# A hybrid decoder layer on one core: the delta rule's products and output turn in another order, w_out's gate on another engine, and a PSUM pool of its own for the last norm

## The chip, the core and the metric

The kernel runs on one core of a Trainium2 chip. The core has five engines, each with an instruction queue of its own that it works through in order: TensorE (PE in the profile; PEld is its weight load), VectorE (DVE), ScalarE (ACT), GpSimd (POOL) and SyncE (SP), which here issues most of the transfers (DMA). [...] The metric is device time in microseconds of one execution, as a median of runs.

## The reference, cut to what matters

One layer over 2048 tokens of width 1024: a combined projection, two mixers (a short convolution and a gated delta rule with 4 heads of 128), an output product with w_out, a layer norm, 32 experts of which each token takes two, and a last layer norm. All in float32.

```python
h = x * (1 + scale1) + shift1
proj = h @ w_in                       # 1024 x 3592
y_conv = short_conv_mixer(...)        # 512 columns
y_dn = gated_deltanet(...)            # 512 columns: the delta rule below, then RMS norm, times silu(z)
x = layer_norm(ALPHA * x + gate1 * (concat(y_conv, y_dn) @ w_out), ln1_g, ln1_b)
x = layer_norm(ALPHA * x + gate2 * hierarchical_moe(x * (1 + scale2) + shift2), ln2_g, ln2_b)

def step(S, xs):                      # one chunk of the delta rule, for each head
    delta = u_c - w_c @ S
    o = qd_c @ S + qk_c @ delta
    S = S * dec_c + ke_c^T @ delta
    return S, o
```

## The kernel before, in words

The mixer works in two halves of 1024 tokens. In each half the projections run column tile by column tile (`qkv_tile`, `z_tile`, `conv_group`); each product is split in three fp32r matmuls (line 283). The delta rule's 16 chunks of 128 tokens go by generators that `drive` steps beside the projections: each `yield` of the main line lets a side generator make a fixed share of a step (0.6 in the first half, 1.0 in the second). `gdn` runs `gdn_a` for the half's 8 chunks, then an inversion (`gdn_inv`, `gdn_merge`), then `gdn_b` chunk by chunk, which carries the state S. The second half's chunks run on beside `mix_tile`, which makes the w_out product and the first norm for 128 tokens at a time; `main` makes it wait until `gdn_done` has passed its chunk.

Outside the blocks marked `manual_schedule`, the order in which the code is written gives each instruction a rank, and a planner, which knows costs and due times of its own, puts the instructions of each engine in their final order before anything runs. So two generators' instructions are mixed on each queue, and an instruction can be planned well ahead of its place. Buffers are given out by the planner too: the tiles of `t2` share 11 buffers (m2), the PSUM tiles of `gps` share 4 banks.

In `gdn_b` a chunk loads six tiles (kTb, qTb, Tm, qkb, keb, veb) and later szb. For each head, PE makes pr = k S (line 719), and DVE forms r in veb from it (line 720). PE multiplies T by r into pdl (line 723), ACT scales that to e in Tm (line 726), PE makes ke e into pS (line 730) and DVE the new state from it (line 732). The output o in qTb is q S (line 739, ACT line 741) plus qk e (line 745, DVE line 748). Then follow a sum of squares on ACT (line 754), a chain of small DVE instructions for the root (lines 755 to 759), a scaling of qTb (line 761), four transposes on PE into oT (line 768), a product with szb on DVE (line 769) and a store (line 770). Lines 719 and 720 alternate by head within one PSUM bank, and so do lines 730 and 732.

`load_wout` loads w_out in eight pieces, multiplies each by the gate on POOL (line 827) and splits it on ACT and DVE (lines 828 and 829). This runs beside the last `conv_group` of the second half and the first tiles of the mix.

`moe` runs the experts under an order written by hand for all engines. Its PSUM tiles come from the pools ph (1 bank) and pk (7 banks), which stay open to the end. `tail` is the last norm over 16 tiles of 128 tokens, in six groups (`TAIL`); only SP's order is by hand there. For each tile, ACT normalises the columns from TS on (line 1649), POOL multiplies and adds the norm's rows there (line 1657), and DVE does all of the first TS columns in two instructions (line 1656), with the rows g and b taken from PSUM (the banks of pT, 512 columns each, filled at line 1585). TS is 512.

Of the kernel before, what the change touches and what calls it, by code (L numbers as in the profile page):

```python
# [10 lines left out]
F32 = mybir.dt.float32  # L11
# [5 lines left out]
OP = mybir.AluOpType  # L17
# [3 lines left out]
P = 128  # L21
D = 1024
# [5 lines left out]
H = 4  # L28
# [7 lines left out]
NG = 4  # L36
NONE = 1 << 20
ADA = 0.4
TS, TAIL = 512, ((1, 1), (2, 1), (3, 1), (4, 1), (3, 1), (3, 1))
HS = 608  # L40

RA, RB, MH2, MH3, WO = 0.6, 1.0, 0.25, 0.5, 0.5
# [7 lines left out]
def dram(ap, offset, dims):  # L50
    return bass.AP(tensor=ap.tensor, offset=ap.offset + offset, ap=[list(d) for d in dims])


class Layer:
# [647 lines left out]
    def gdn_b(self, ci):  # L702
# [13 lines left out]
        if ci:  # L716
            pr = self.gps("pr")
            for h in range(H):
                nc.tensor.matmul(pr[:, h * P:(h + 1) * P], kT[:, h], S[:, h], start=True, stop=True)
                nc.vector.scalar_tensor_tensor(r[:, h], pr[:, h * P:(h + 1) * P], self.neg_eg[:, ci, h:h + 1], r[:, h], op0=OP.mult, op1=OP.add)  # L720
            yield
        for h in range(H):
            nc.tensor.matmul(pd[:, h * P:(h + 1) * P], T[:, h], r[:, h], start=True, stop=True)
        e = T
# [3 lines left out]
        pS = self.gps("pS")  # L728
        for h in range(H):
            nc.tensor.matmul(pS[:, h * P:(h + 1) * P], ke[:, h], e[:, h], start=True, stop=True)  # L730
            if ci:
                nc.vector.scalar_tensor_tensor(Sn[:, h], S[:, h], self.dec[:, ci, h:h + 1], pS[:, h * P:(h + 1) * P], op0=OP.mult, op1=OP.add)
            else:
                nc.vector.tensor_copy(Sn[:, h], pS[:, h * P:(h + 1) * P])
# [27 lines left out]
        sz = self.t2((P, H, P), name="szb")  # L762
        q, off = divmod(ci, 4)
        nc.sync.dma_start(sz, dram(self.szT[q], off * P, [[QW, P], [P * QW, H], [1, P]]))
        yield
        pT = self.gps("oT")
        for h in range(H):
            nc.tensor.transpose(pT[:, h * P:(h + 1) * P], o[:, h], self.ident)
        nc.vector.scalar_tensor_tensor(fl(sz), pT, self.dnw, fl(sz), op0=OP.mult, op1=OP.mult)
        nc.sync.dma_start(dram(self.yT[q], 4 * P * QW + off * P, [[QW, P], [P * QW, H], [1, P]]), sz)  # L770
        yield

    def scratch(self):
# [40 lines left out]
    def load_wout(self):  # L814

        nc, I = self.nc, self.I
        g1 = self.xp.tile([P, D], F32, tag="x", name="gate1")
        self.row(g1, self.d_mod, 0)
        self.wo = []
        for n in range(2):  # L820
            c = slice(n * 512, n * 512 + 512)
            lo = self.t16([P, KD, 512], F32R, name="wo_lo")
            hi = self.t16([P, KD, 512], F32R, name="wo_hi")
            for k in range(0, KD, 2):
                r = self.raw4((P, 2, 512), name="wo_raw")
                nc.sync.dma_start(r, dram(I["w_out"], k * P * D + n * 512, [[D, P], [P * D, 2], [1, 512]]))
                nc.gpsimd.tensor_tensor(r, r, g1[:, None, c].to_broadcast([P, 2, 512]), op=OP.mult)
                nc.scalar.activation(hi[:, k:k + 2], r, AF.Copy)
                nc.vector.tensor_tensor(lo[:, k:k + 2], r, hi[:, k:k + 2].bitcast(F32), op=OP.subtract)
                yield  # L830
            self.wo.append((hi, lo))
            while not self.second:
                yield
# [327 lines left out]
    def moe_pools(self, st):  # L1161
        p = lambda **k: self.pool(st, **k)
        self.raws.append(p(name="raw8b", bufs=3))
        self.yp = p(name="yp", bufs=3)
        self.xtp = p(name="xtp", bufs=2)
        self.hp = p(name="hp", bufs=3)
        self.hrp = p(name="hrp", bufs=2)
        self.mc = p(name="mc", bufs=1)
        self.small = p(name="small2", bufs=2)
        self.ph = p(name="ph", bufs=1, space=PSUM)  # L1170
        self.pk = p(name="pk", bufs=1, space=PSUM)

    def load_up(self, e):

# [400 lines left out]
    def tail(self):  # L1575
# [4 lines left out]
        junk, stats = (self.hrp.tile([P, D], F32, tag="hr", name=n) for n in ("junk", "stats"))  # L1580
        xs, groups = [], []

        rows = [t.rearrange("p a b -> p (a b)") for t in self.pTs]
        for t, r in zip(rows, (g, b)):
            act.activation(t, r[:, 0:TS], AF.Copy)
        for i in range(NT // 4):
# [3 lines left out]
                nc.sync.dma_start(x[:, j], self.d_xa[t * P:(t + 1) * P])  # L1590
                xs.append(x[:, j])

        t, cols = 0, self.pgs[0]
        for n, nv in TAIL:
            f = stats[:, 64 * len(groups):64 * len(groups) + 64]
            c = cols[:, 16 * len(groups):16 * len(groups) + 16]
# [145 lines left out]
    def gdn(self, half):  # L1742
        c0 = 8 * half
        for c in range(8):
            yield from self.gdn_a(c0 + c)
        yield from self.gdn_inv(half)
        yield from self.gdn_merge(c0)
        for c in range(c0, c0 + 8):
            yield from self.gdn_b(c)
            self.gdn_done = c + 1  # L1750
            if c % 2 == 0 and c < c0 + 6:
                yield from self.gdn_merge(c + 2)

    def step(self, x):
        try:
# [2 lines left out]
            self.sides.remove(x)  # L1758

    def drive(self):  # L1760
        self.sides, self.later, self.gdn_done = [], [], 0
        for _ in self.main():
            for x in list(self.sides):
                x.append(x.pop() if len(x) > 2 else 0.0)
# [7 lines left out]
    def run(self):  # L1772
# [16 lines left out]
        with self.late as st:  # L1789
            self.moe_pools(st)  # L1790
            E = mybir.EngineType
            with self.tc.manual_schedule(engines={E.PE, E.Activation, E.DVE, E.Pool, E.SP}):
                self.moe()
            with self.tc.manual_schedule(engines={mybir.EngineType.SP}):
                self.tail()


# [17 lines left out]
```

## Time and profile before

| what | value |
|---|---|
| median of 3 runs | 1762.85 us (1756.54, 1763.17, 1762.85) |
| profiled execution | 1759.53 us |
| its span, first to last instruction | 1757.8 us |
| mean granted clock of TensorE | 0.954 |
| busy: PE, DVE, ACT, POOL | 88%, 72%, 44%, 31% |
| mixer, to the last mix tile | 0 to about 1163 us |
| experts | about 1193 to 1674 us |
| last norm | about 1674 to 1757.8 us |

Busy time is an average over these stages. A wait is the idle time of an engine ahead of an instruction, with the instruction that ended it. [...]

### The profile page before, as it was taken

What the parts mean: (1) busy time and instruction counts of PE and PEld (TensorE: products, weight loads), DVE (VectorE), ACT (ScalarE), POOL (GpSimd) and SP (SyncE); (2) the same over time, 40 slices, a digit from 0 to 9 for tenths busy, and PEclk for the clock granted to TensorE, in tenths of its full rate; (3) what the DMA queues carried; (4) which work ended last, traced back from release to release, by engine and by line L of the source; (5) the groups of instructions that cost most, each with busy time, mean ns of one, the idle gap of its engine ahead of it and who ended that gap; (6) DMA issues with size and microseconds to landing.
All of it is one profiled execution on the core that took longest, in us unless ns stands there. A gap on an engine that the chain in (4) does not pass through costs nothing. (4 is left out here: it accounts for less than half of the span.)

```text
span 1757.8 us, 25239 instructions
## 1 busy us (share of the span) xinstructions
PE 1555.2 (88%) x7786; PEld 1265.9 (72%) x7786; DVE 1259.4 (72%) x3042; ACT 774.6 (44%) x1604; POOL 537.5 (31%) x442
## 2 busy tenths in 40 slices
PE   5899999998999999999789999958999989999800
PEld 4678877877777778888668888846777778778600
DVE  6777667766877987684678878786666786776554
ACT  4433445445233336444443332235545565554452
POOL 3200111021110002122321121225656675765427
PEclk9999999999999999999899999978999999999955
DMA  9553586456765758544477764449989998998464
GB/s 282 168 184 102 165 248 198 128 138 164 211 202 149 216 162 249 147 98 121 134 231 222 238 204 145 139 150 269 291 256 289 289 327 253 299 300 243 107 221 179
DMA packets 348006, 356.79 MB, mean 203 GB/s; under 512 B 49745, under 2 KB 283842, under 8 KB 347858
## 3 DMA queue, kind: packets, MB, share of 16 engines
q1 hardware_dynamic: 330610, 316.63, 57.4%
q0 software_dynamic: 17248, 38.37, 9.1%
q8 instruction: 70, 1.15, 0.3%
q14 instruction: 78, 0.64, 0.1%
HBM read 268.84 MB, written 101.79 MB: 211 GB/s over the span
## 5 line engine op out<-in xcount | busy, mean ns | idle before, releaser
L283 PE MATMUL acc<-hhi,w_hi 128*128 128x512 f32 x896 | 363.2, 406 | 7.8 <-ACT st L447 3.4
L283 PE MATMUL acc<-hlo,w_hi 128*128 128x512 f32 x896 | 358.2, 400 | 2.3 <-DVE hlo L340 1.3
L283 PE MATMUL acc<-hhi,w_lo 128*128 128x512 f32 x896 | 359.1, 401 | 0.0
L283 PEld LDWEIGHTS acc<-hhi,w_hi 128*128 128x128 f32 x896 | 172.1, 192 | 45.4 <-ACT st L447 4.4
L283 PEld LDWEIGHTS acc<-hlo,w_hi 128*128 128x128 f32 x896 | 171.7, 192 | 38.1 <-DVE hlo L340 2.7
L283 PEld LDWEIGHTS acc<-hhi,w_lo 128*128 128x128 f32 x896 | 172.0, 192 | 35.9 <-issue 1.7
L1223 POOL TENSOR_TENSOR dn<-dn_raw,dn 128x1024 fp32r<-128x1024 f32 x64 | 168.3, 2659 | 59.3 <-ACT dn L1222 57.0
L1214 DVE TENSOR_TENSOR gu_lo<-gu_raw,gu_hi 128x1024 fp32r<-128x1024 f32 (+1 forms) x128 | 172.8, 1393 | 15.4 <-ACT gu_hi L1213 8.5
L1256 PE MATMUL pg<-gu_hi,xT_hi 128*128 128x512 f32 x376 | 150.0, 399 | 0.7 <-ACT xT_hi L1246 0.5
L1256 PE MATMUL pg<-gu_hi,xT_lo 128*128 128x512 f32 x376 | 147.5, 392 | 0.1
L1256 PE MATMUL pg<-gu_lo,xT_hi 128*128 128x512 f32 x376 | 147.2, 392 | 0.0
L1289 PE MATMUL pd<-dn,hT_hi 128*128 128x512 f32 x376 | 120.7, 402 | 6.3 <-PEq L1332 3.2
L1213 ACT ACTIVATE gu_hi<-gu_raw 128x1024 fp32r<-128x1024 f32 (+1 forms) x128 | 125.1, 1035 | 1.9
L456 DVE SCALAR_TENSOR_TENSOR cv<-st,cw,cv 128x512 f32<-128x512 f32 x144 | 108.6, 754 | 2.0
L1303 POOL DMA_INDIRECT d_xa<-y,idx x47 | 77.0, 1638 | 103.8 <-DVEq L1332 44.2
L917 PE MATMUL mix<-wo_hi,y_hi 128*128 128x512 f32 x256 | 104.1, 407 | 1.3 <-ACT y_hi L876 1.3
L917 PE MATMUL mix<-wo_hi,y_lo 128*128 128x512 f32 x256 | 103.2, 403 | 1.3 <-DVE y_lo L878 1.3
L917 PE MATMUL mix<-wo_lo,y_hi 128*128 128x512 f32 x256 | 102.0, 398 | 0.0
L350 ACT ACTIVATE w_hi<-raw 128x1024 fp32r<-128x1024 f32 x56 | 59.6, 1065 | 89.2 <-PE acc L283 70.4
L1247 DVE TENSOR_TENSOR xT_lo<-pT,xT_hi 128x512 fp32r<-128x512 f32 x94 | 60.6, 686 | 40.0 <-ACT xT_hi L1246 34.5
L578 POOL TENSOR_SCALAR_AFFINE_SELECT gam<-gam 128x512 f32<-128x512 f32 x16 | 10.8, 675 | 250.0 <-ACT gam L577 202.7
L1289 PEld LDWEIGHTS pd<-dn,hT_hi 128*128 128x128 f32 x376 | 67.1, 188 | 27.4 <-issue 7.0
(364 smaller groups left out, 3276.8 us busy)
## 6 DMA issues: line engine op xcount, KB each, us to landing
dn_raw<-in_w_down_dram SPq DMA_DIRECT2D x32, 1024.0 KB
gu_raw<-in_w_gate_dram SPq DMA_DIRECT2D x60, 512.0 KB
gu_raw<-in_w_up_dram SPq DMA_DIRECT2D x60, 512.0 KB
raw<-in_w_in_dram SPq DMA_DIRECT2D x56, 512.0 KB
ada_w<-in_w_ada_dram SPq DMA_DIRECT2D x96, 256.0 KB
qkvT<-cv SPq DMA_DIRECT2D x48, 256.0 KB
x_t<-in_x_dram SPq DMA_DIRECT2D x16, 512.0 KB
y_raw<-yT SPq DMA_DIRECT2D x16, 512.0 KB
```

The source lines that it names most:

```text
L283: self.nc.tensor.matmul(ps, a[:, k, :], b[q][:, k, :], start=k + n == 0, stop=k == KD - 1 and n == 2)
L350: nc.scalar.activation(hi, raw, AF.Copy)
L456: nc.vector.scalar_tensor_tensor(y, st[:, t:t + 512], self.cw4[:, j, t:t + 1], y, op0=OP.mult, op1=OP.add)
L578: nc.gpsimd.affine_select(gam, gam, pattern=[[0, H], [1, P]], compare_op=OP.is_ge, fill=0.0, base=0, channel_multiplier=-1)
L917: self.nc.tensor.matmul(ps, a[:, k, :], self.wo[n][b][:, k, :], start=k + i == 0, stop=k == KD - 1 and i == 2)
L1213: nc.scalar.activation(hi[:, c], r, AF.Copy)
L1214: i = nc.vector.tensor_tensor(lo[:, c], r, hi[:, c].bitcast(F32), op=OP.subtract)
L1223: nc.gpsimd.tensor_tensor(dn[:, 1, k], r[:, k], dn[:, 0, k].bitcast(F32), op=OP.subtract)
L1247: nc.vector.tensor_tensor(lo[:, c], pT[n], hi[:, c].bitcast(F32), op=OP.subtract)
L1256: self.nc.tensor.matmul(ps, a[:, k], b[:, k], start=n == 0, stop=n == 3 * KD - 1)
L1289: self.nc.tensor.matmul(ps[n], hT[a][:, k], dn[:, b, k, c], start=i == 0, stop=i == 5)
L1303: i = self.nc.gpsimd.indirect_dma_start(out=self.d_xa, out_offset=bass.IndirectOffsetOnAxis(ap=idx[:, 0:1], axis=0), in_=y, in_offset=None ...
```

## The change

It has five parts. In `gdn_b` the four heads' products of lines 719 and 730 are written together, ahead of the four DVE instructions that read them. The output turn (transposes, product, store) becomes a function that is put on a list; the next chunk calls it after its own pr and ahead of pdl, and the half's last one is called at the end of `gdn`; the mark `gdn_done` is set inside it. `gdn` makes 4 (first half) or 2 (second half) empty steps ahead of its first `gdn_b`. `load_wout` multiplies by the gate on DVE instead of POOL. And the pools ph and pk are closed after `moe`; the last norm takes its rows (two banks each) and its small columns (one bank) from a PSUM pool of its own, with TS 704 instead of 512.

```diff
-TS, TAIL = 512, ((1, 1), (2, 1), (3, 1), (4, 1), (3, 1), (3, 1))
+TS, TAIL = 704, ((1, 1), (2, 1), (3, 1), (4, 1), (3, 1), (3, 1))
...
             for h in range(H):
                 nc.tensor.matmul(pr[:, h * P:(h + 1) * P], kT[:, h], S[:, h], start=True, stop=True)
+            for h in range(H):
                 nc.vector.scalar_tensor_tensor(r[:, h], pr[:, h * P:(h + 1) * P], self.neg_eg[:, ci, h:h + 1], r[:, h], op0=OP.mult, op1=OP.add)
             yield
+        while self.gdn_out:
+            self.gdn_out.pop()()
         for h in range(H):
             nc.tensor.matmul(pd[:, h * P:(h + 1) * P], T[:, h], r[:, h], start=True, stop=True)
...
         for h in range(H):
             nc.tensor.matmul(pS[:, h * P:(h + 1) * P], ke[:, h], e[:, h], start=True, stop=True)
+        for h in range(H):
             if ci:
                 nc.vector.scalar_tensor_tensor(Sn[:, h], S[:, h], self.dec[:, ci, h:h + 1], pS[:, h * P:(h + 1) * P], op0=OP.mult, op1=OP.add)
...
-        yield
-        pT = self.gps("oT")
-        for h in range(H):
-            nc.tensor.transpose(pT[:, h * P:(h + 1) * P], o[:, h], self.ident)
-        nc.vector.scalar_tensor_tensor(fl(sz), pT, self.dnw, fl(sz), op0=OP.mult, op1=OP.mult)
-        nc.sync.dma_start(dram(self.yT[q], 4 * P * QW + off * P, [[QW, P], [P * QW, H], [1, P]]), sz)
+
+        def out():
+            pT = self.gps("oT")
+            for h in range(H):
+                nc.tensor.transpose(pT[:, h * P:(h + 1) * P], o[:, h], self.ident)
+            nc.vector.scalar_tensor_tensor(fl(sz), pT, self.dnw, fl(sz), op0=OP.mult, op1=OP.mult)
+            nc.sync.dma_start(dram(self.yT[q], 4 * P * QW + off * P, [[QW, P], [P * QW, H], [1, P]]), sz)
+            self.gdn_done = ci + 1
+        self.gdn_out.append(out)
         yield
...
-                nc.gpsimd.tensor_tensor(r, r, g1[:, None, c].to_broadcast([P, 2, 512]), op=OP.mult)
+                nc.vector.tensor_tensor(r, r, g1[:, None, c].to_broadcast([P, 2, 512]), op=OP.mult)
...
-        rows = [t.rearrange("p a b -> p (a b)") for t in self.pTs]
+        rows = [self.pk.tile([P, D], F32, name=f"row{i}")[:, 0:TS] for i in range(2)]
...
-        t, cols = 0, self.pgs[0]
+        t, cols = 0, self.pk.tile([P, 512], F32, name="cols")
...
         yield from self.gdn_merge(c0)
+
+        for _ in range(4 if half == 0 else 2):
+            yield
         for c in range(c0, c0 + 8):
             yield from self.gdn_b(c)
-            self.gdn_done = c + 1
             if c % 2 == 0 and c < c0 + 6:
                 yield from self.gdn_merge(c + 2)
+        while self.gdn_out:
+            self.gdn_out.pop()()
...
-            with self.tc.manual_schedule(engines={E.PE, E.Activation, E.DVE, E.Pool, E.SP}):
-                self.moe()
-            with self.tc.manual_schedule(engines={mybir.EngineType.SP}):
+            with ExitStack() as banks:
+                self.ph = self.pool(banks, name="ph", bufs=1, space=PSUM)
+                self.pk = self.pool(banks, name="pk", bufs=1, space=PSUM)
+                with self.tc.manual_schedule(engines={E.PE, E.Activation, E.DVE, E.Pool, E.SP}):
+                    self.moe()
+            self.pk = self.pool(st, name="pt", bufs=1, space=PSUM)
+            with self.tc.manual_schedule(engines={E.SP}):
                 self.tail()
```

## Rows read from the trace of the kernel before

**Rows 1.** The page, part 1: busy us, share of span, instructions.

```profile
PE 1555.2 (88%) x7786; PEld 1265.9 (72%) x7786; DVE 1259.4 (72%) x3042; ACT 774.6 (44%) x1604; POOL 537.5 (31%) x442
```

**Rows 2.** Stretches: length; busy PE, PEld, DVE, ACT, POOL; PE clock, DMA share, GB/s.

```profile
420.00:660.00 240.00, 225.57 (x1173) 179.16 (x1173) 196.99 (x528) 86.31 (x242) 20.75 (x29) 0.98 0.65 189
...
830.00:905.00 75.00, 60.35 (x281) 48.89 (x281) 50.17 (x96) 32.01 (x61) 26.01 (x18) 0.86 0.54 160
...
1200.00:1674.00 474.00, 447.28 (x2141) 359.38 (x2139) 324.98 (x401) 254.53 (x369) 290.71 (x152) 1.00 0.86 267
...
1702.00:1757.80 55.80, 0.00 (x0) 0.00 (x0) 30.93 (x112) 24.27 (x38) 39.59 (x32) 0.50 0.43 173
```

**Rows 3.** PE's waits, whole span: us in total, times, longest.

```profile
PE oT L768 <- DVE qTb L761: 11.6, 8, 4.2
...
PE pS L730 <- DVE S L732: 4.6, 3, 3.3
...
PE pr L719 <- DVE veb L720: 2.9, 3, 1.9
PE pdl L723 <- DMA veb<-d_ve: 2.3, 1, 2.3
```

**Rows 4.** The same view, 420 to 660 us only.

```profile
PE oT L768 <- DVE qTb L761: 6.1, 6, 2.5
```

**Rows 5.** Timeline of PE, 830 to 870: start, length, instructions, [idle before, its end].

```profile
838.44 0.49 PE L719 MATMUL pr<-S,kTb 128*128 128x128 f32 x2 [1.89 <-DVE veb L720]
...
850.51 0.79 PE L730 MATMUL pS<-Tm,keb 128*128 128x128 f32 x2 [3.28 <-DVE S L732]
...
863.66 0.37 PE L768 MATMUL oT<-ident,qTb 128*128 128x128 f32 x1 [4.18 <-DVE qTb L761]
```

**Rows 6.** Timelines of POOL and of DVE in the same stretch.

```profile
833.18 2.41 POOL L827 TENSOR_TENSOR wo_raw<-wo_raw,gate 128x1024 f32<-128x1024 f32 x1 [0.84 <-DMA wo_raw<-in_w_out_dram]
...
844.46 4.66 POOL L827 TENSOR_TENSOR wo_raw<-wo_raw,gate 128x1024 f32<-128x1024 f32 x2 [2.99 <-DMA wo_raw<-in_w_out_dram]
858.77 4.75 POOL L827 TENSOR_TENSOR wo_raw<-wo_raw,gate 128x1024 f32<-128x1024 f32 x2 [9.65 <-DVE rst L124]
...
833.47 3.21 DVE L829 TENSOR_TENSOR wo_lo<-wo_raw,wo_hi 128x1024 fp32r<-128x1024 f32 x1 [3.39 <-ACT wo_hi L828]
...
846.76 2.65 DVE L490 TENSOR_SCALAR cy<-st,cw 128x512 f32<-128x512 f32 x1
...
858.92 2.24 DVE L759 TENSOR_TENSOR om<-ors,aq 128x4 f32<-128x4 f32 x1
...
882.76 0.48 DVE L490 TENSOR_SCALAR cy<-st,cw 128x512 f32<-128x512 f32 x1
```

**Rows 7.** Groups by line: busy us, mean ns, idle before with releasers.

```profile
L352 DVE TENSOR_TENSOR w_lo<-raw,w_hi 128x1024 fp32r<-128x1024 f32 x52 | 63.5, 1222 | 18.4 <-ACT w_hi L350 17.3 <-PE xT L327 1.0
```

**Rows 8.** Lines L768 and L917: shortest, median, longest ns; first and last start.

```profile
L768 PE MATMUL oT<-ident,qTb x64: 270/327/477, 438.8 to 1045.0; 128*128 128x128 f32 x64
...
L917 PE MATMUL mix<-wo_hi,y_lo x256: 387/389/628, 893.3 to 1163.2; 128*128 128x512 f32 x128
```

**Rows 9.** Timelines of POOL and DVE in the last norm.

```profile
1719.15 32.42 POOL L1657 TENSOR_TENSOR tail_x<-tail_x,ln 128x512 f32<-128x512 f32 x26 [3.36 <-ACT tail_x L1649]
...
1733.14 0.15 DVE L1644 TENSOR_TENSOR stats<-pg,stats 128x3 f32<-128x3 f32 x1
```

**Rows 10.** Groups by line, as in rows 7.

```profile
L809 POOL TENSOR_TENSOR rows<-rows,rowt 128x1024 f32<-128x1024 f32 x1 | 2.4, 2399 | 9.9 <-DVE rowt L807 9.9
...
L1657 POOL TENSOR_TENSOR tail_x<-tail_x,ln 128x512 f32<-128x512 f32 x32 | 39.6, 1264 | 36.2 <-DMA tail_x<-d_xa 26.6 <-ACT tail_x L1649 9.0
L1656 DVE SCALAR_TENSOR_TENSOR tail_x<-tail_x,stats,pT 128x512 f32<-128x512 f32 x32 | 23.3, 736 | 0.1
L1649 ACT ACTIVATE tail_x<-tail_x,stats 128x512 f32<-128x512 f32 x16 | 11.9, 802 | 7.7 <-DVE stats L1644 7.7
```

**Rows 11.** Waits of SP's queue, 420 to 660 us.

```profile
SPq L712 <- PE oT L768: 2.9, 1, 2.9
```

More of the change, by code (lines that the diff above doesn't have):

```diff
@@ L1169, in moe_pools @@
         self.small = p(name="small2", bufs=2)
-        self.ph = p(name="ph", bufs=1, space=PSUM)
-        self.pk = p(name="pk", bufs=1, space=PSUM)
     def load_up(self, e):
@@ L1760, in drive @@
     def drive(self):
-        self.sides, self.later, self.gdn_done = [], [], 0
+        self.sides, self.later, self.gdn_done, self.gdn_out = [], [], 0, []
         for _ in self.main():
```

## The prediction, made before the change was run

> **What bounds the kernel now.** I read the page's busy line first, then stretches of the span, then what TensorE (PE) waited for inside them, then the timeline around those waits. PE is busy 88% of the span [rows 1], so a microsecond is won only where PE stands still or runs at the lower clock, or where there is no PE work. The table of stretches [rows 2] shows four places. From 420 to 660 us (delta rule of the first half, between projections) PE is busy 225.57 of 240 us, clock 0.98. From 830 to 905 us (end of the projections, w_out prepared, first chunks of the second half) it is busy 60.35 of 75 us, and the mean granted clock is 0.86: the worst stretch of the mixer. The experts (1200 to 1674) are not touched. In the last norm (1702 to the end) PE does nothing and GpSimd (POOL) is the busiest engine, 39.59 of 55.8 us.
>
> What PE waited for over the whole span [rows 3] names the change's lines: the output turn oT for qTb of VectorE (DVE) 11.6 us, pS for S 4.6, pr for veb 2.9, pdl for a load of veb 2.3. Of these, oT 6.1 falls between 420 and 660 [rows 4]; the three largest of the other stretch are single waits, of pr 1.89, of pS 3.28 and of oT 4.18 us, 9.4 together [rows 5].
>
> **Why those three are so long.** Beside each runs a gate multiplication of w_out on POOL, and a DVE instruction that is far too long [rows 6]: w_lo's counterpart wo_lo 3.21 us beside POOL's op of 833.18; a 128x512 tensor_scalar 2.65 us beside those of 844.46, where the same line takes 0.48 at 882.76; a 128x4 product 2.24 us beside those of 858.77. So DVE stood about 2.0 to 2.2 us behind POOL each time, and PE, in order, stood behind DVE. [...]
>
> **The change, part by part.** The sum is made against the profiled execution, 1759.53 us (span 1757.8 and 1.7 around it); the median of the three runs, 1762.85, is 3.3 above it, and I add that back at the end.
>
> *Gate to DVE.* POOL loses 8 ops; DVE gains 8. Their price is bounded by wo_lo's cousin w_lo, the same 128x1024 tensor_tensor, 1.222 us [rows 7]: 9.8 us. It loses the stalls, three shown at 2.0, 2.2 and 2.1, 6.3 us: net DVE +3.5 us, in a stretch where DVE is busy 50.17 of 75 us. Gain: the three waits, 9.4 us. Clock: 0.14 x 60.35 = 8.4 us is lost in the stretch; 9.4 of its 14.65 us idle are these waits, so 64% of it, 5.4 us, goes with them. I charge all of DVE's net work to PE: 9.4 + 5.4 - 3.5 = 11.3 us. The ends are 4 us (half of the waits stay, since the order changes anyway and the delta rule's own ping-pong was part of them) and 17.8 us (waits and clock, all of it). The second half of w_out is late only against the first mix product, which waits for it at the stretch's end; a shorter gate helps there, and I count nothing for it.
>
> [...]
>
> *State products together, pr and pS.* Four pairs of matmuls run in one go, then four DVE products, instead of PE and DVE by turns in one PSUM bank. No instruction is added. For pS the next reader of the state is a chunk away, so its wait is gone: 4.6 less the 3.28 that is in the gate's term, 1.3 us. For pr what is late next is pdl, which needs veb; I count pr's wait as gone, 2.9 less 1.89, 1.0 us.
>
> *Output turn late.* The 16 output turns (4 transposes, one 128x512 DVE product, one store on SP each) move behind the next chunk's pr. PE's 6.1 us before oT in the first half go, but DVE was 82% busy there (196.99 of 240 [rows 2]), and the next thing queued on PE, pdl, waits for a DVE product behind the same queue. I keep half: 3 us. In the second half 1.3 us beyond the three waits are left (11.6 - 6.1 - 4.18): 1 us. The store passes six loads of a chunk on the SP queue; y is only read by the mix, and the last turn ends at 1045 us against a mix that runs to 1163 [rows 8], so the late done mark costs nothing; if that cover were gone, one turn would lie open, four transposes of 0.33 us and a store.
>
> *Yields before the first chunk.* 4 and 2 steps more for the merge's stores to land. Half of the 2.3 us wait for veb: 1.2 us. Nobody waits for the delay, by the same cover.
>
> Together, put down to the first half: 1.3 + 1.0 + 3 + 1.2 = 6.5 us of its 14.4 idle; of its clock loss, 0.02 x 225.57 = 4.5 us, the same share, 2.0: 8.5 us. Ends 0 and 15 (all named waits and clock).
>
> *Last norm.* DVE takes 704 columns instead of 512, POOL and ScalarE (ACT) 320. POOL's final run is 26 ops in 32.42 us, 1.247 each, back to back to the end [rows 9]. POOL ops of 1024 and 512 columns take 2.399 and 1.264 us [rows 10]: 2.22 ns a column, so 192 columns less make 0.43 less, 0.82 a step. DVE's product takes 0.736; against 1.222 for 1024 columns [rows 7] that is 0.95 ns a column, +0.18 us each. Of its 32, 30 stand ahead of the last scale at 1733.14 [rows 9]: +5.5, so 1738.6; then ACT's first of that group, at its old 0.8 [rows 10] and 0.2 for its start, 1739.6; six POOL ops, 1744.5, where POOL now ends at 1751.6. Gain 7.1 us; the ends are 1.5 (a wide PSUM read across two banks costs double, no row shows one) and 7.8 (POOL bound: 26 x 0.82 = 21.3 from a start 3.2 us later, as 18 of the 32 wide products stand ahead of it). The two row copies and the new PSUM pool come ahead of loads that are waited for anyway: nothing; if that cover is gone, 0.4 us for 384 more columns at 0.95 ns.
>
> [...]
>
> Sum: 11.3 + 8.5 + 1 + 7.1 = 27.9. 1759.5 - 27.9 = 1731.6; with 3.3 back to the median, 1735.
>
> **The rivals.** (a) The wait moves: DVE's queue stays as late as it is, and PE meets it at pdl instead of oT. For: DVE's 82% and pdl directly behind. Against: between pr and pdl now stand transposes and projections. Then only pS, the gate's lower end and the last norm count: 4 + 1.3 + 7.1 = 12.4, time 1750. (b) The planner undoes it: it orders by readiness and due times, so the mixer's waits just land elsewhere and only the last norm stands: 1762.85 - 7.1 = 1756. (c) Slower, by held buffers: qTb and szb of a chunk now live into the next one, in a ring of 11 tiles of which a chunk uses 7, so the next chunk's loads start later and PE meets them as it met veb, 2.3 us [rows 3]. For: SP's load of T already waited for an oT to free its buffer [rows 11], 2.9 us. Against: that was one wait, and it did not reach PE. At all 14 chunk boundaries it costs 32.6 us against the 18.4 us of gate and norm that remain: 1777. It decides from 8 of 14 boundaries on.
>
> **How the numbers follow.** Forecast 0.62, (a) 0.18, (b) 0.12, (c) 0.08, for the rows show the gate's stalls plainly and the first half's less so. A measurement of this kernel can tell some 0.5%, 8.8 us, from no change: 1754.0 is the bound. The forecast's own ends: 4 + 0 + 0 + 1.5 = 5.5 less and 17.8 + 15 + 1.2 + 7.8 = 41.8 less, that is 1757 and 1721; both corners are unlikely at once. The range takes in (a) and (b) and leaves (c) out: 1718 to 1758. Faster: 0.62 less 0.02 for its weak corner, (a) 0.15 of its 0.18, (b) 0.03: 0.78. Same: 0.14. Slower: (c), 0.08.
>
> **What would show it.** Right: gate rows on DVE near 1.2 us, no DVE op above 2 us between 820 and 900, clock above 0.93 there; no wait of PE for qTb above 1 us; pr in runs of eight without veb between; POOL's last run ended by ACT, not back to back, at near 0.82 us. (a) shows as pdl waiting for veb by over 8 us, (b) as PE idle unchanged at near 29 us over both stretches, (c) as PE waits for loads named kTb, Tm or veb. I am wrong in size if the clock stays at 0.86 with the waits gone, or if 704 columns take over 1.1 us.

## The result, and the profile after

The changed kernel takes 1737.82 us (median; 1733.45 to 1740.98), the kernel before, timed beside it, 1759.82 (1756.54 to 1763.17). The ratio is 0.9873 with a 95% interval of 0.984 to 0.9907: 1.3% or 22.0 us faster. Timed once more in another series, the same two kernels gave 0.9902 (0.9869 to 0.9934). The profiled execution of after took 1740.98 us, span 1739.3, mean granted clock (TensorE's, as a share of full speed) 0.956.

| | predicted | measured |
|---|---|---|
| time after, us | 1735, range 1718 to 1758 | 1737.82 |
| gain against the start it was counted from | 27.9 of 1759.5 | 22.0 of 1759.82 |
| more than 0.5% faster | chance 0.78 | yes |

The forecast's number is 2.8 us off, and that is in part luck: its sum was 5.9 too large, and it had added 3.3 us back to reach a median of 1762.85, which with more runs came down by 3.0. By the first timing the gain lies between 16.4 and 28.2 us, so that 27.9 is just inside; by the second it is 17.2 us (11.6 to 23.0), and 27.9 is outside. The rest of this text is about those 5.9 us and about which part earned what.

The busy line of the page of after, to be read beside [rows 1]: PE 6.3 us less busy, POOL 34.0 less, DVE 6.2 less although the gate is now its work.

```profile
PE 1548.9 (89%) x7786; PEld 1269.3 (73%) x7786; DVE 1253.2 (72%) x3050; ACT 771.1 (44%) x1604; POOL 503.5 (29%) x434
```

The stretches of after, columns as in [rows 2], with one more stretch, 905 to 1050:

```profile
420.00:660.00 240.00, 228.34 (x1222) 187.39 (x1222) 199.52 (x553) 92.60 (x272) 22.86 (x32) 0.99 0.66 200
830.00:905.00 75.00, 67.08 (x391) 58.35 (x392) 55.61 (x174) 32.77 (x88) 10.48 (x18) 0.91 0.71 207
905.00:1050.00 145.00, 138.69 (x788) 117.95 (x787) 114.39 (x404) 46.48 (x124) 20.79 (x34) 0.96 0.65 205
```

and that extra stretch of the kernel before:

```profile
905.00:1050.00 145.00, 142.30 (x871) 121.52 (x870) 121.96 (x452) 51.40 (x153) 20.80 (x34) 1.00 0.77 232
```

Where the change was made, 830 to 905, PE is 6.7 us busier and the clock is up from 0.86 to 0.91. Right behind it, 905 to 1050, PE is 3.6 us less busy and the clock is down from 1.00 to 0.96. Part of what the first stretch wins seems to be given back in the next. (After runs about 10 us ahead of before here, so the two windows don't hold quite the same work.)

PE's waits over the whole span of after, columns as in [rows 3]:

```profile
PE oT L773 <- DVE qTb L765: 15.2, 7, 4.6
PE pdl L726 <- DVE veb L721: 2.6, 1, 2.6
PE pdl L726 <- DMA veb<-d_ve: 2.2, 1, 2.2
```

The waits of pr for veb and of pS for S are gone, as the regrouping should have it. The wait of oT for qTb, which the late turn was to shorten, went up from 11.6 to 15.2 us. Read alone, these rows say that 7.5 us of waits became 6.2 others, which can't explain 22 us.

**Where one execution ends its stages.** Three last starts cut the span into four: the last z tile (end of the first half's delta rule and of the second half's first projections), the last product of the mix, the last expert product. The views by line, of before and then of after (shortest, median, longest ns; first and last start; the mix's row of before is in [rows 8]):

```profile
L468 ACT ACTIVATE zs<-acc x16: 578/614/662, 198.5 to 720.9; 128x512 f32<-128x512 f32 x16
L1289 PE MATMUL pd<-dn,hT_lo x188: 388/393/398, 1211.8 to 1672.9; 128*128 128x512 f32 x188
```

```profile
L468 ACT ACTIVATE zs<-acc x16: 577/613/655, 197.1 to 710.6; 128x512 f32<-128x512 f32 x16
L924 PE MATMUL mix<-wo_hi,y_lo x256: 387/389/774, 884.3 to 1151.0; 128*128 128x512 f32 x128
L1294 PE MATMUL pd<-dn,hT_lo x188: 388/393/398, 1199.2 to 1659.9; 128*128 128x512 f32 x188
```

To the last z, after is 10.3 us ahead; from there to the last mix product 1.9 more (442.3 became 440.4); the experts 0.8 (509.7, 508.9); the last norm 5.5 (84.9, 79.4). By this one pair the gate, the largest term of the sum, brought next to nothing. The gate measured alone shows that this reading is wrong, and the second execution below shows why a single pair misleads.

### The profile page after: what moved, and what is told of

It reads as the page before. It is cut to its first block, busy times and chain, and to the rows that moved or that the text cites. A ratio compares the mean times of both kernels' runs of the same rounds, so it can differ in the third digit from the quotient of the medians.

```text
span 1739.3 us, 25241 instructions
## 1 busy us (share of the span) xinstructions
PE 1548.9 (89%) x7786; PEld 1269.3 (73%) x7786; DVE 1253.2 (72%) x3050; ACT 771.1 (44%) x1604; POOL 503.5 (29%) x434
## 5 line engine op out<-in xcount | busy, mean ns | idle before, releaser
L283 PE MATMUL acc<-hhi,w_lo 128*128 128x512 f32 x896 | 355.4, 397 | 0.0
L1219 DVE TENSOR_TENSOR gu_lo<-gu_raw,gu_hi 128x1024 fp32r<-128x1024 f32 (+1 forms) x128 | 172.9, 1394 | 15.2 <-ACT gu_hi L1218 9.0
L458 ACT ACTIVATE th<-cv 128x512 f32<-128x512 f32 x48 | 30.3, 632 | 131.1 <-DVE cv L456 131.1
```

The source lines that it names most:

```text
L283: self.nc.tensor.matmul(ps, a[:, k, :], b[q][:, k, :], start=k + n == 0, stop=k == KD - 1 and n == 2)
L458: nc.scalar.activation(th, y, AF.Tanh)
L1219: i = nc.vector.tensor_tensor(lo[:, c], r, hi[:, c].bitcast(F32), op=OP.subtract)
```

## The experiments

Each part alone on the kernel before, then each part taken out of the changed kernel, then the disputed costs. The table has the median, the ratio to the kernel before timed in the same series, and the stages of the profiled execution read as above (last z; z to mix; expert end to span end). Go by the ratio between series: the kernel before itself had medians of 1759.82, 1751.86, 1754.69 and 1755.15 us in the four of them.

| kernel | us | ratio, 95% | last z | to mix | norm |
|---|---|---|---|---|---|
| before | | 1 | 720.9 | 442.3 | 84.9 |
| last norm alone | 1748.14 | 0.9976 (0.9954, 0.9998) | 719.0 | 438.8 | 78.8 |
| gate alone | 1742.76 | 0.9943 (0.9919, 0.9967) | 715.5 | 430.3 | 86.4 |
| products alone | 1759.90 | 1.0046 (1.0025, 1.0067) | 715.2 | 446.3 | 85.4 |
| late turn alone | 1743.79 | 0.9946 (0.9924, 0.9968) | 705.2 | 438.6 | 85.9 |
| after | 1737.82 | 0.9873 (0.9840, 0.9907) | 710.6 | 440.4 | 79.4 |
| after, again | 1737.56 | 0.9902 (0.9869, 0.9934) | 709.8 | 433.8 | 79.6 |
| after, products apart | 1732.76 | 0.9885 (0.9850, 0.9920) | 707.5 | 431.1 | 79.0 |
| after, turn early | 1740.15 | 0.9925 (0.9897, 0.9953) | 720.0 | 434.7 | 79.0 |
| after, gate on POOL | 1739.65 | 0.9910 (0.9874, 0.9945) | 707.0 | 444.7 | 79.3 |
| after, no extra yields | 1734.51 | 0.9886 (0.9847, 0.9925) | 716.0 | 435.7 | 79.2 |
| after, only pr apart | 1737.67 | 0.9912 (0.9878, 0.9945) | 708.1 | 440.1 | 79.2 |
| after, turn still later | 1731.59 | 0.9874 (0.9841, 0.9907) | 706.0 | 434.5 | 79.0 |

### The parts alone

**The last norm.** The edit is the diff's lines on TS, `rows`, `cols` and the pools, nothing else.

> The kernel before with the last norm's part alone (TS 704, rows and columns in a PSUM pool of their own). Theory A, the parts add and the norm's is worth what its own stage shows in the changed kernel: from the end of the experts' last product to the last GpSimd operation the changed kernel is 5.6 us shorter, so 5 to 6 us faster, 0.3%. Theory B, a part of that stage's gain is owed to what runs ahead of it: under 3 us. By the prediction's sum 7.1 us.

Measured 0.9976, 4.2 us (0.4 to 8.1). The rows of after show what its pieces cost; first the groups by line (busy us, mean ns | idle before), then POOL's timeline:

```profile
L1661 DVE SCALAR_TENSOR_TENSOR tail_x<-tail_x,stats,row 128x704 f32<-128x704 f32 x32 | 29.7, 935 | 0.8 <-ACT junk L1617 0.7
L1662 POOL TENSOR_TENSOR tail_x<-tail_x,ln 128x320 f32<-128x320 f32 x32 | 27.0, 860 | 43.1 <-DVE cols L1627 28.1 <-ACT tail_x L1654 13.8
```

```profile
1709.83 5.30 POOL L1662 TENSOR_TENSOR tail_x<-tail_x,ln 128x320 f32<-128x320 f32 x6 [3.42 <-ACT tail_x L1654]
1715.41 17.60 POOL L1662 TENSOR_TENSOR tail_x<-tail_x,ln 128x320 f32<-128x320 f32 x20 [0.29 <-ACT tail_x L1654]
```

DVE's wide product takes 935 ns, the prediction had 0.736 + 0.18 = 0.916; POOL's takes 860 ns and comes every 0.88 us (17.60 / 20), the prediction had 0.82. In the table, the four executions with TS 512 need 84.9 to 86.4 us from the last expert product to the end (mean 85.7), the nine with 704 need 78.8 to 79.6 (mean 79.2). No kernel of one kind lies near one of the other: 6.5 us, inside the timed interval. So theory A stands by the stages; the timing by itself leaves both open.

**The gate.**

```diff
-                nc.gpsimd.tensor_tensor(r, r, g1[:, None, c].to_broadcast([P, 2, 512]), op=OP.mult)
+                nc.vector.tensor_tensor(r, r, g1[:, None, c].to_broadcast([P, 2, 512]), op=OP.mult)
```

> The kernel before with w_out's gate on VectorE and nothing else. Theory A, as predicted: the three long waits of TensorE near 838, 850 and 864 us go, 4 to 18 us faster, 11 at the middle, and no VectorE instruction of the stretch takes over 2 us. Theory B, TensorE's waits there come from VectorE's lateness in general and land elsewhere: within 4 us of before, TensorE's idle time from 830 to 1050 us again 15 to 18 us.

Measured 0.9943, 10.0 us (5.8 to 14.2), against a term of 11.3. Its stretches, to be read beside [rows 2] and the extra stretch above, its waits over the whole span, and the busy line of its page:

```profile
830.00:905.00 75.00, 65.52 (x342) 53.09 (x341) 58.31 (x137) 37.10 (x79) 8.19 (x11) 0.95 0.69 206
905.00:1050.00 145.00, 144.80 (x875) 122.86 (x874) 122.10 (x471) 47.56 (x144) 24.68 (x41) 1.00 0.72 219
```

```profile
PE oT L768 <- DVE qTb L761: 5.9, 7, 1.9
PE pr L719 <- DVE veb L720: 3.9, 4, 2.3
```

```profile
PE 1547.1 (89%) x7786; PEld 1257.5 (72%) x7786; DVE 1257.4 (72%) x3050; ACT 774.7 (45%) x1604; POOL 516.1 (30%) x434
```

The three long waits of [rows 5] are gone (the longest of oT is 1.9 where it was 4.2) and the clock is 0.95 instead of 0.86; behind it, in 905 to 1050, it stays at 1.00. PE's idle time over 830 to 1050 fell from 17.4 to 9.7 us, where theory B had 15 to 18. Cause and effect stand where the prediction put them. One sign of theory A missed: a DVE product of the norm's rows (line 808) took 3.39 us at 893.21, beside POOL's product for the same rows (line 809), which ran from 893.16 for 2.34 us. So the holds beside the gate are gone, and one beside another POOL instruction is there.

**The state products together.**

```diff
                 nc.tensor.matmul(pr[:, h * P:(h + 1) * P], kT[:, h], S[:, h], start=True, stop=True)
+            for h in range(H):
...
             nc.tensor.matmul(pS[:, h * P:(h + 1) * P], ke[:, h], e[:, h], start=True, stop=True)
+        for h in range(H):
```

> The kernel before with the four heads' products of pr and of pS written together and nothing else. Theory A, as predicted: only the waits of pr and pS go, 2 to 3 us faster. Theory B, the shorter chain of a chunk is what lets the chunks follow each other faster (18 to 19 us apart in the changed kernel's second half against 24 before) and brings most of the first half's gain: 6 to 12 us faster, chunks closer together, and the wait of the output turn stays or grows.

Measured 1.0046 (1.0025 to 1.0067): about 8 us slower, where the sum had a gain of 2.3. In the trace the waits of pr and pS are gone, and oT's has grown:

```profile
PE oT L770 <- DVE qTb L763: 16.0, 10, 4.9
```

One place shows how. The timelines of PE, DVE and POOL in this kernel, around 853 us:

```profile
853.95 0.69 PE L770 MATMUL oT<-ident,qTb 128*128 128x128 f32 x2 [4.65 <-DVE qTb L763]
```

```profile
851.35 2.22 DVE L761 TENSOR_TENSOR om<-ors,aq 128x4 f32<-128x4 f32 x1
853.61 2.97 DVE L763 TENSOR_SCALAR qTb<-qTb,om 128x128 f32<-128x128 f32 x4
```

```profile
851.22 2.34 POOL L829 TENSOR_TENSOR wo_raw<-wo_raw,gate 128x1024 f32<-128x1024 f32 x1 [6.25 <-DVE rst L124]
853.86 2.45 POOL L829 TENSOR_TENSOR wo_raw<-wo_raw,gate 128x1024 f32<-128x1024 f32 x1 [0.30 <-DMA wo_raw<-in_w_out_dram]
```

DVE is held by POOL's gate as before: a 4-column product takes 2.22 us, and four scalings that take 0.87 us elsewhere take 2.97. PE, freed of its waits at pr, pS, meets the same late DVE one step on, at oT. Grouping removed the place of the wait, not its cause. Neither theory had a loss. Why the time is even 8 us longer is not settled: from z to mix this execution took 446.3 us, the longest of all, but to the last z it was 5.7 us ahead; and its own time, 1755.70, is below that of the profiled execution of before, so that this pair doesn't show the loss.

The clock is a likely part of it. Right behind the projections PE has one more long wait at oT, 4.91 us, and over 905 to 1050 the granted clock was 0.94, where before had 1.00:

```profile
906.76 0.47 PE L770 MATMUL oT<-ident,qTb 128*128 128x128 f32 x1 [4.91 <-DVE qTb L763]
```

```profile
905.00:1050.00 145.00, 139.82 (x813) 121.08 (x814) 112.13 (x422) 44.82 (x134) 24.18 (x37) 0.94 0.69 210
```

Other executions agree: in 905 to 1050 the granted clock is 1.00 in five in which both products alternate with DVE (before, gate alone, late turn alone, after with products apart, no gate at all), and 0.94 to 0.99 in seven in which pr, pS or both are grouped (0.94 products alone, 0.96 after, 0.98 after again, 0.96 turn early, 0.95 gate on POOL, 0.97 only pr apart, 0.99 turn still later). With products alone PE stood 4.91 us at one go just ahead of 907, in after 4.58 just ahead of 904.4; in before no wait of PE between 895 and 1050 is above 1.96 us. With 0.91 in 830 to 905, products alone lost 0.09 x 61.38 + 0.06 x 139.82 = 13.9 us to the clock where before lost 0.14 x 60.35 = 8.4: an estimated 5.5 us more.

**The late turn.** The diff's lines on `out`, `gdn_out` and `gdn_done`, with products alternating and the gate on POOL.

> The kernel before with the output turn late and nothing else. Theory A, as predicted: TensorE's wait ahead of the turn shrinks from 11.6 us to half, 3 to 5 us faster. Theory B, the planner puts the turn back to the moment at which it believes qTb ready, so that the wait stays at 10 us or more: within 3 us of before.

Measured 0.9946, 9.5 us (5.6 to 13.3). Its waits over the span:

```profile
PE pr L719 <- DVE veb L720: 10.2, 9, 4.4
PE oT L771 <- DVE qTb L763: 3.4, 4, 1.7
```

oT's wait fell from 11.6 to 3.4 us, and pr's rose from 2.9 to 10.2. As above the wait went to the next product that needs DVE; but here the time fell, and by more than theory A's 3 to 5 us. So the sum of the named waits is no measure of the time.

Singly the four come to 4.2 + 10.0 + 9.5 - 8.1 = 15.6 us; the whole was 22.0, and 17.2 when timed again.

### The parts taken out

**Products apart again.** The diff of the products above, backwards, on the changed kernel.

> The changed kernel with the state products alternating with DVE's additions again, as before; all else as changed. By the theory that the parts add (products alone read 1.0046 of the time before) this is faster than the changed kernel: 0.983 of before, and the trace has waits of pr and pS back (about 1.9 and 3.3 us in 830 to 905) but less of oT than the 15.2 us of the changed kernel. By the rival that the grouped products pay only together with the late turn (the parts measured alone sum to 15.7 us, the whole to 22.3, and the missing 6.6 us is theirs) it is 0.986 to 0.987, no faster than the changed kernel.

Measured 0.9885: no different from the changed kernel (0.9873 and 0.9902). So the theory that the parts add (0.983) fell, and the rival held in that the products cost nothing in company; that they pay there is not shown. Its waits show pr and pS back and oT gone, as the expectation had it:

```profile
PE pr L719 <- DVE veb L720: 8.1, 6, 2.3
PE pS L732 <- DVE S L734: 5.7, 5, 2.0
...
PE oT L771 <- DVE qTb L763: 0.5, 2, 0.3
```

8.1 + 5.7 + 0.5 = 14.3 us against 15.2 at oT in after, and 11.5 in its second execution below: PE waits about as long for DVE in either order, as far as single executions tell.

**The turn early.** The turn back behind po, in its own chunk.

> The changed kernel with the output's turn back in its own chunk, behind po; all else as changed. If the parts add, the turn is worth what it was worth alone, 9.5 us: 0.9927 of before. By the rival (grouped products need the late turn) it loses 16 us: 0.9965, with an oT wait above the 16.0 us that grouped products alone showed.

Measured 0.9925, and 7.1 us (3.2 to 11.0) above the kernel with products apart of the same series. Additive parts said 0.9927, the rival 0.9965 with an oT wait above 16.0; the wait was 13.1. (That kernel differs from this one in two parts, the products and the turn. Beside the kernel without yields, of the same series too, it is 5.1 us slower, with an interval of 0.7 faster to 10.9 slower.) The rival fell: grouped products don't need the late turn. What the turn is worth in company lies at 4 to 9 us by these runs.

This run and the next one also show when the products cost their 8 us. Here the norm and the gate, 14.2 us by themselves, are in, and 13.2 (8.2 to 18.1) was measured; in the next the norm and the turn, 13.7 us, and 15.8 (9.6 to 22.1) was measured. Another 8 us off would put both sums below these intervals. The sums have errors of their own, so this is an indication: grouping was seen to cost 8 us where the gate was on POOL and the turn early, and with either of the two changed the cost is not seen.

**The gate on POOL again.**

> The changed kernel with w_out's gate multiplication on GpSimd again; all else as changed. If the parts add it loses 10 us: 0.993 of before, with stretched DVE operations (over 2 us) and pr or oT waits again between 820 and 900 us. By the rival, that the late turn had already covered those waits (the stretch from the last projection to the mix ends only 1.8 us sooner in the changed kernel), it is within 3 us of the changed kernel: 0.988 to 0.989.

Measured 0.9910, between the two expectations of 0.993 and 0.988 to 0.989. The stalls are back, at the same DVE instruction that follows below for after; timelines of DVE, POOL and PE:

```profile
860.92 2.41 DVE L509 SCALAR_TENSOR_TENSOR cy<-cy,cnw,cs 128x512 f32<-128x512 f32 x1 [1.71 <-ACT cs L508]
```

```profile
860.44 2.34 POOL L834 TENSOR_TENSOR wo_raw<-wo_raw,gate 128x1024 f32<-128x1024 f32 x1 [0.64 <-DMA wo_raw<-in_w_out_dram]
```

```profile
864.17 0.47 PE L773 MATMUL oT<-ident,qTb 128*128 128x128 f32 x1 [6.20 <-DVE qTb L765]
```

PE waits 6.20 us, 1.71 of which DVE had itself spent waiting for ACT and some 1.7 more standing beside POOL (2.41 against 0.75 in after). In its series this kernel is 5.6 us (1.9 to 9.3) slower than the one with products apart, which differs in the products too, and 3.6 us slower than the one without yields, with an interval of 2.2 faster to 9.4 slower.

**No extra yields.**

> The changed kernel without the extra yields behind the merge of a half (4 and 2); all else as changed. If the 6.6 us by which the whole exceeds its measured parts belong to these yields, this is 0.991 of before; if they belong to grouped products and late turn together, it is 0.987 to 0.988, the same as the changed kernel.

Measured 0.9886, the second expectation: the yields carry nothing that this measurement can tell. Nor did they touch the wait that they were meant for: pdl's wait for the load of veb is 2.3 us before, 2.2 in after and 2.2 here.

### What the waits are worth, and the gate's own work

**The changed kernel once more.**

> The changed kernel itself, unaltered, as the measure for the other runs of this chip: 0.987 of before by its first timing. Its profiled run shows how far a second execution of one program differs in the named waits: if oT for qTb is again 13 to 17 us, the wait belongs to the order of the work; if it is below 9, single profiles can't settle where the time goes.

Measured 0.9902. The profiled execution has these waits:

```profile
PE oT L773 <- DVE qTb L765: 7.2, 5, 3.1
...
PE oT L773 <- DMA rows<-d_mod: 4.3, 1, 4.3
PE pdl L726 <- DVE veb L721: 2.6, 1, 2.6
```

and these stretches:

```profile
830.00:905.00 75.00, 67.43 (x415) 58.73 (x414) 56.79 (x176) 34.32 (x93) 9.85 (x17) 0.98 0.71 212
905.00:1050.00 145.00, 140.40 (x794) 119.03 (x793) 119.20 (x429) 48.07 (x128) 21.72 (x34) 0.98 0.65 207
```

oT for qTb takes 7.2 us where the first execution of the same program had 15.2. Part of that is a matter of names: the wait of 4.3 us that the profile puts down to a load of rows stands at the same pair of products as the one of 4.58 for qTb in after, and DVE's scaling of qTb had begun just ahead of it here too. With it oT has 11.5 us, between the two expectations. The span is 9.0 us shorter, and 6.6 of these lie between z and mix (440.4, 433.8). A single profile can't settle a term of this size; that is why the table's columns are compared in groups below.

**The turn still later.**

```diff
-        while self.gdn_out:
-            self.gdn_out.pop()()
         for h in range(H):
             nc.tensor.matmul(pd[:, h * P:(h + 1) * P], T[:, h], r[:, h], start=True, stop=True)
...
                 nc.vector.tensor_copy(Sn[:, h], pS[:, h * P:(h + 1) * P])
+        while self.gdn_out:
+            self.gdn_out.pop()()
         o = qT
```

> The changed kernel with the output's turn put still later: behind the next chunk's pS and its state products instead of ahead of pdl. Theory: PE waits at oT (15.2 us in the changed kernel) because with grouped products only eight matmuls of pr stand between the chunk's end and the turn; later, oT falls below 5 us and the time by up to 10 us, to 0.982 of before. Rival: DVE's queue is what is late, at 83% busy in 420 to 660, and the wait moves to pdl for veb, pS or pqS, which rise together by about the 10 us that oT loses: 0.987, unchanged.

Measured 0.9874, 1731.59 us beside 1737.56 for the changed kernel in the same series; the difference of the means is 4.8 us with an interval of 0.4 to 9.3. Its waits:

```profile
PE pdl L724 <- DVE veb L721: 6.4, 4, 2.6
...
PE pdl L724 <- DMA inv_op<-d_op: 4.7, 1, 4.7
...
PE oT L773 <- DVE qTb L765: 1.3, 1, 1.3
```

oT is below 5 us, as the theory said. But over all releasers pdl waits 15.6 us where it waited 4.6 in the changed kernel's execution of this series, no less of a rise than what oT lost (11.5 to 1.3); 4.7 us of it is one wait for a load. So the wait moved, as the rival had it, and the ratio is the rival's too. Against the changed kernel of the same series the time still fell, by little.

**Only pr apart.** The products of pr alternate, those of pS stay together.

> The changed kernel with the products of pr alternating with DVE again and those of pS left in one run. Theory: it is pr's run of matmuls that brings PE to oT too early; alternated, oT is below 8 us, pr waits for veb about 8 us, pS not at all (it was 5.7 with both apart), and the time is 0.984 of before. Rival: the sum of the waits stays near 15 us whatever the grouping, 0.987.

Measured 0.9912 (1737.67 us, beside 1737.56 for the changed kernel of the series). The theory's 0.984 fell. The rival has it right that the time doesn't change, but not its sum:

```profile
PE pr L719 <- DVE veb L720: 16.1, 12, 2.3
...
PE oT L772 <- DVE qTb L764: 5.3, 1, 5.3
```

oT has one wait of 5.3 us left and pr 16.1, together 21.4 and not 15. How pr is grouped moved the place at which PE meets DVE and left the time where it was.

**No gate at all.** The kernel before without its line 827.

> The kernel before without the multiplication of w_out by its gate on any engine (that part of the computation is left out); all else as before. If the eight multiplications on VectorE, 9.8 us, lie on TensorE's path, this is faster than the gate on VectorE alone (0.9943) by about as much: 0.989. If VectorE has room for them and the whole gain is the end of the stalls beside GpSimd, it is the same as that kernel: 0.993 to 0.995.

Its time, 1899.75 us, is of no use, and the run missed both expectations for a reason that neither had thought of: without the gate x is another, tokens go to other experts, and PE waits for rows (ov_hr) of the block that the kernel runs only when some expert has more than 256 tokens. Up to the mix the work is the same, so the last mix product can be read, here and in the kernel with the gate alone on DVE:

```profile
PE pT L1236 <- DMA ov_hr<-d_h,ove: 139.0, 3, 49.9
```

```profile
L916 PE MATMUL mix<-wo_hi,y_lo x256: 387/389/484, 877.2 to 1139.8; 128*128 128x512 f32 x128
```

```profile
L917 PE MATMUL mix<-wo_hi,y_lo x256: 387/389/497, 870.4 to 1145.8; 128*128 128x512 f32 x128
```

From the last z to there it is 422.5 us without the gate, 430.3 with it on DVE, 442.3 with it on POOL. By these three single executions most of the gate's 9.8 us on DVE (eight of 1.222) lies on PE's path, 7.8 us, and moving it still pays. But two executions of one program differed by 6.6 us in this stage (440.4 and 433.8), so the 7.8 is an indication and not a measure.

## Why the prediction was right, and where it was not

**What bounds the stretch: right.** The gate's rows on DVE are as costed, and no instruction of DVE between 820 and 905 is above 1.25 us in after. The group by line:

```profile
L834 DVE TENSOR_TENSOR wo_raw<-wo_raw,gate 128x1024 f32<-128x1024 f32 x8 | 9.8, 1222 | 3.4 <-DMA wo_raw<-in_w_out_dram 3.3
```

The longest gate instruction of after is 1.227 us. No instruction of POOL ran beside any of the eight, so whether POOL would hold one is not shown.

**The gate's term: right alone, and its clock not always kept in company.** Alone it gave 10.0 us for 11.3, and its pieces came out in its one profile. PE's idle time in 830 to 905 fell from 14.65 to 9.48 us, 5.2 for a net 5.9 (9.4 less 3.5); the clock's loss there fell from 8.4 to 0.05 x 65.52 = 3.3, 5.1 for 5.4. One item was too dear: DVE's total is 1257.4 us against 1259.4 before, with 9.8 of gate in it, so that 11.8 us of its other time went away, where the prediction counted three holds, 6.3, and charged 3.5 net to PE. In the whole change the clock's win was kept in one execution of two. Clock lost over 830 to 1050 in after: 0.09 x 67.08 + 0.04 x 138.69 = 11.6 us, against 8.4 before; when run again (0.98 of 67.43 and of 140.40) 4.2. So the clock's share there was between 3.2 us lost and 4.2 won. By the clocks of 905 to 1050 given above, what takes it back goes with the grouped products and not with the gate; why it does is not shown.

**The first half: right in sum, wrong in its pieces.** The table's last z is 715.2 to 720.9 us in the five kernels with the early turn (mean 718.1) and 705.2 to 716.0 in the eight with the late one (mean 708.8): 9.3 us for a term of 8.5. But the term put 3 us on the turn, 2.3 on the products, 1.2 on the yields and 2.0 on the clock. With the turn early and all the rest changed, the last z stands at 720.0, where it was. It is the turn that earns it; halving its gain because DVE was 82% busy was the mis-sized step. (The kernel without yields, with 716.0 the latest of the eight, doesn't speak for the yields: the turn alone has none either and is the earliest, 705.2.) Not all of it is won for good: the wait moved on in part, as rival (a) had it (pdl for veb 2.6 us, not the 8 it named).

**The products: the step that failed.** "For pS the next reader of the state is a chunk away, so its wait is gone", and for pr likewise, 2.3 us. The rows were gone and the waits were not; alone the part cost 8 us, in company nothing that shows. What was overlooked is that all of these products wait for one engine, DVE, in one queue: take PE past the first of them and it stands at the next, in fewer and longer waits (the longest between 895 and 910 is 4.91 us with products alone), and the clock was lower in the stretch behind, 0.94 against 1.00.

**Adding the parts: probably too much, not shown.** The gate and the late turn were summed as if they removed different waits. The last mix product by kernel, means of the profiled executions:

| | gate on POOL | gate on DVE |
|---|---|---|
| turn early | 1160.8 (1163.2, 1157.8, 1161.5) | 1150.3 (1145.8, 1154.7) |
| turn late | 1147.8 (1143.8, 1151.7) | 1145.6 (six, 1138.6 to 1151.7) |

Alone the gate wins 10.5 us and the late turn 13.0; together 15.2. Executions within one cell differ by up to 13.1 us, so the overlap of 8.3 is uncertain by itself. The times lean the same way without settling it. The gate is worth 10.0 us by itself, and putting it back on POOL in the changed kernel costs 0.9910 less 0.9873 or 0.9902, 6.5 or 1.4 us; the turn is worth 9.5 us by itself, and 9.1 or 4.0 taken out (0.9925 less the same two). Each of these differences has an interval of some 8 us either way. A likely reason, argued and not shown, is that the late turn gives PE transposes to do ahead of the product that a held DVE delays, so that fewer of POOL's stalls reach PE. To the mix's end the sum had 11.3 + 8.5 + 1 = 20.8 us, and 15.2 are shown; the norm had 7.1, and 6.5 are. 15.2 + 6.5 = 21.7 is the 22.0 measured: nearly all of the excess of 5.9 us lies ahead of the mix's end. How it divides there stays open. The products and the yields, 3.5 us of the sum, brought nothing, the turn brought more than its 4 us, and the gate's clock was kept in one execution of two.

**The last norm: right.** 6.5 for 7.1, and POOL, not DVE, bounds its end, since POOL's instruction is 0.04 to 0.06 us longer than a straight line through 1024 and 512 columns gave; over 26 that is 1.0 to 1.6 us. POOL's last run starts behind ACT, but its 20 instructions are then back to back, which the sign had ruled out. The 704 columns across two banks take 0.935 us on DVE in the profile, near the 0.916 that the prediction worked out from its rows; DVE starts its next instruction 0.85 to 0.87 us after such a one in the five from 1698.59 to 1702.70, of which this is one:

```profile
1701.72 0.94 DVE L1661 SCALAR_TENSOR_TENSOR tail_x<-tail_x,stats,row 128x704 f32<-128x704 f32 x1
1702.57 0.16 DVE L1632 TENSOR_SCALAR cols<-stats 128x2 f32<-128x2 f32 x1
```

The term's lower end, 1.5 us, supposed that a read across two banks costs double; no run shows such a cost, and the 0.935 us stands in its place.

**The signs named in advance.** Wrong: "no wait of PE for qTb above 1 us". Half right: "clock above 0.93", which was 0.91 in after, 0.98 in its second execution and 0.95 with the gate alone. One wait of after shows why the first could not hold. Timelines of PE, DVE and ACT around 900 us:

```profile
904.38 0.48 PE L773 MATMUL oT<-ident,qTb 128*128 128x128 f32 x1 [4.58 <-DVE qTb L765]
```

```profile
900.65 0.75 DVE L509 SCALAR_TENSOR_TENSOR cy<-cy,cnw,cs 128x512 f32<-128x512 f32 x1 [2.49 <-ACT cs L508]
...
904.04 0.87 DVE L765 TENSOR_SCALAR qTb<-qTb,om 128x128 f32<-128x128 f32 x4
```

```profile
896.70 1.28 ACT L507 ACT_TABLE_LOAD   x1
...
898.70 1.28 ACT L508 ACT_TABLE_LOAD   x1
```

PE waits for DVE's scaling of qTb; DVE stood 2.49 us at a row of the other mixer, cy, ahead of the root's chain; cy waited for ACT, which loaded two tables of 1.28 us for it. No gate and no long instruction of POOL is in it. The wait belongs to the order of DVE's queue, at which no part of the change aims.

**The rivals.** (b), that the planner undoes it, and (c), held buffers, show no sign: PE's idle time over both stretches fell from 29.1 to 19.6 us (11.66 + 7.92), and no wait of PE for a load names kTb or Tm; the one for a load of veb is 2.2 us where it was 2.3.

## What to carry to other kernels

When an engine waits in several places for one other engine, regrouping its products can move the wait without shortening it: here, alone, it took the waits of pr and pS (2.9 and 4.6 us) away, oT's rose from 11.6 to 16.0, and the kernel was about 8 us slower. Remove what makes the other engine late, or give the waiting one other work, and be slow to add up the two, since both may pay for the same waits (here 10.5 and 13.0 us to the mix's end, each alone, and 15.2 together). Before you trust a stage's gain, look at a second execution: here one program had 15.2 us of a named wait and then 7.2 (11.5 with the part that went by another name), and its span differed by 9.0 us, and only groups of executions, stage by stage, agreed with the times. Moving work off an engine can pay even at the price of a busier one, where the first engine held that one (2.0 to 2.2 us at a time beside POOL's gate products): the gate's eight products take 9.8 us of DVE, and the kernel with that change alone is 10.0 us faster.

## What the runs showed of the hardware that was not expected

- The hold by POOL was no shorter for a small instruction: a 128x4 product took 2.22 us (with products alone; 0.16 in after, where no POOL product ran beside it) and a 128x512 one 2.41 (gate on POOL again; 0.75 in after), beside POOL products of 2.34 us each.
- ACT loaded a table twice within 3.3 us, 1.28 us each, for a logarithm and the exponential behind it (lines 507 and 508, an inverse square root), and it was felt two engines on: DVE stood 2.49 us for it, within PE's chain to the wait of 4.58 us at 904.38.
- The granted clock differed with the grouping of the small products: in 905 to 1050 it was 1.00 in the five executions above with both alternating and 0.94 to 0.99 in the seven others, in two of which PE had stood 4.58 (after) and 4.91 us (products alone) at one go at the start of that stretch. No run here changes these single waits alone, so that the one comes from the other is not shown.
